# Which units of the first feed-forward network have a slab split for the mixer beside them

## The chip, the cores and the metric

One Trainium2 chip; the program runs on 1 of its cores. The metric is the device time in microseconds (us) of that core, and lower is better. Engines are named as in the profile: PE is TensorE's matrix multiply, PEld its weight load, DVE is VectorE, ACT is ScalarE, POOL is GpSimd, SP is the engine whose queue issues most DMA loads. An engine works through its instructions in the order in which they stand in its program; an instruction that waits holds up those behind it.

## The reference, cut to what matters

One decoder layer on 512 tokens of width 1024, all in float32: a feed-forward half-step (FFN1), a mixer, a second feed-forward half-step (FFN2), a final norm.

```python
x = x + 0.5 * ffn(rmsnorm(x, ffn1_norm), ffn1_w_gate, ffn1_w_up, ffn1_w_down)
x = x + hybrid_mixer(rmsnorm(x, mix_norm), w_in, ..., w_out)
x = x + 0.5 * ffn(rmsnorm(x, ffn2_norm), ffn2_w_gate, ffn2_w_up, ffn2_w_down)
y = rmsnorm(x, final_norm)

def swiglu_ffn(x, w_gate, w_up, w_down):     # w_gate, w_up: 1024x2816, w_down: 2816x1024
    return (silu(x @ w_gate) * (x @ w_up)) @ w_down
```

The mixer multiplies by `w_in` (1024x2048) and `w_out` (1024x1024); what lies between the two does not matter here.

## The kernel before

**Split operands.** Every operand of a product is kept as a rounded part `hi` and a rest `lo`, and every product is three matmuls: hi by hi, hi by lo, lo by hi. A weight slab (128x1024) is loaded as `raw` by SP (L177), cast to `hi` by ACT (L203 or L238), and `lo = raw - hi` is made by DVE (L212). Four `raw` and five `hl` buffers turn over.

**The two feed-forward networks.** The 2816 hidden features are 22 tiles of 128, in groups of 8, 8 and 6 (L21). For each tile j the gate and the up product are made together from seven block products (`seven_units`, L452), each a unit of 12 matmuls that are 256 columns wide; the first tiles are made plainly. The two weight slabs of a pair (gate, up) also give two tiles `tt` of differences (DVE, L226 to L230), so a pair needs four `hl` tiles. The first unit of a pair leaves its product in a PSUM bank; ACT copies it out (L473) and only then the third unit may add to that bank. After each of the first two groups come its down products (`down_a_units`, L538): 8 units, 4 for each half of the output, 24 matmuls of 512 columns each. The last group's down products are `down_b_units` (L564) in FFN1.

**Splits for the mixer.** The mixer's 24 weight slabs (16 of `w_in`, 8 of `w_out`) are split during FFN1, while its own weights stream in, and written to DRAM as hi and lo, from where the mixer loads them later. This is the generator `split_ahead` (L284), which is advanced one step at a time. Step 0 loads slab 0; step n casts slab n-1 on ACT (L290), subtracts on DVE (L291), issues two stores from POOL (L292, L293) and the load of slab n from SP (L296). Loads and halves take their buffers from a pool of 13 (`ACT_BUFS`) that also holds the activations of the group.

```python
for src in srcs[:1] + srcs:                                   # L286
    if raws:
        hi, lo = slot([P, D], "shi", F32R), slot([P, D], "slo", F32R)
        S.copy(hi, raws[-1])                                  # L290, ACT
        V.tensor_sub(lo, raws[-1], hi.bitcast(F32))           # L291, DVE
        G.dma_start(dst[:, 0, :], hi.bitcast(F32))            # L292, POOL queue
        G.dma_start(dst[:, 1, :], lo.bitcast(F32))            # L293
    if len(raws) < len(srcs):
        raws.append(slot([P, D], "sraw"))
        nc.sync.dma_start(raws[-1], srcs[len(raws) - 1])      # L296, SP queue
    yield 1
```

**What sets the order.** `run` (L240) walks a list of units. After each unit that is marked `aside` it advances the generator by one step, with a priority of -400 (L275 to L279); the tile framework then fixes each engine's order from priorities when the kernel is built. Marked are, from tile j = 2 on: the two plain units of j = 2; the fifth unit of each pair whose j is in `BESIDE` (L29, L961); all 8 units of a group's down products (L558, the last argument of `Unit`); and the first 6 units of `down_b_units`. FFN2 runs through the same functions, but the generator is spent by then. 25 steps and one call that ends it are needed; FFN1 before has 31 marked units, so the last ones do nothing.

Of the kernel before, what the change touches and what calls it, by code (L numbers as in the profile page):

```python
# [25 lines left out]
ACT_BUFS = 13  # L26
AHEAD = (8, 4, 3)
PLAIN = (3, 2)
BESIDE = (5, 9, 11, 13, 15, 18, 20)  # L29
ASIDE = 16  # L30
TAPS = 31
PR_NORM = 800
# [40 lines left out]
def layer_kernel(ctx: ExitStack, tc, x, gains, w_g1, w_u1, w_d1a, w_d1b, w_in,  # L73
# [19 lines left out]
    def bank(name):  # L93
        return pb.tile([P, T], F32, name=nm(name), tag="pb")
# [424 lines left out]
    def mm_tok(ps, ahi, alo, whi, wlo, first, last):  # L519
        PE.matmul(ps, ahi, whi, start=first, stop=False)  # L520
        PE.matmul(ps, ahi, wlo, start=False, stop=False)  # L521
        PE.matmul(ps, alo, whi, start=False, stop=last)  # L522

    def add_res(t, oh, ps, scale):
        sl = xt[t][:, oh * 512:(oh + 1) * 512]
        V.scalar_tensor_tensor(out=sl, in0=ps, scalar=scale, in1=sl,
                               op0=ALU.mult, op1=ALU.add)
        dve(0.66)

    def cols(oh):  # L530
        return slice(oh * 512, (oh + 1) * 512)

    def toks(t):
        return slice(t * P, (t + 1) * P)
# [3 lines left out]
    def down_a_units(wd, acts, n):  # L538
        box = {}

        def unit(oh, kp, s):
            if kp == 0:
                box["ps"] = [bank("pd") for _ in range(4)]
            for j in range(2):
                k = 2 * kp + j
                for t in range(4):
                    mm_tok(box["ps"][t], acts[k][:, 0, toks(t)], acts[k][:, 1, toks(t)],
                           s.hi[:, cols(j)], s.lo[:, cols(j)], k == 0, k == n - 1)

        def fin(oh):  # L550
            for t in range(4):
                add_res(t, oh, box["ps"][t], 0.5)

        out_ = []
        for oh in range(2):
            for kp in range(n // 2):
                s = Slab(wd[oh, kp])
                out_.append(Unit([s], 5.44, lambda oh=oh, kp=kp, s=s: unit(oh, kp, s),  # L558
                                 (lambda oh=oh: fin(oh)) if kp == n // 2 - 1 else None, True))
        return out_  # L560


# [377 lines left out]
    def ffn(a0, wg, wu, wd, q, plain, between=()):  # L940
# [8 lines left out]
        for gi, n in enumerate(GROUPS):  # L949
            for i in range(n):  # L950
                j = next(js)
                if j < 2:
                    continue
                if j < plain:
                    put(ffn_units(acts[gi], i, wg[j], wu[j], [ALL]), 1)
                    continue
                if not ready:
                    us.extend(wait(q["name"]))
                    ready = True
                m = seven_units(acts[gi], i, wg[j], wu[j], q)  # L960
                m[4].aside = j in BESIDE  # L961
                if j == FT - 1:
                    put([m[k] for k in (0, 1, 2, 3, 5, 4, 6)], 1)
                else:
                    put(m[:6], 2)
                    late.append(m[6])
            if gi < 2:
                put(down_a_units(wd[gi], acts[gi], n), 1)
            if gi == 0:
                us.extend(between)  # L970
# [129 lines left out]
```

## Time and profile before

| | us |
|---|---|
| median of 3 runs | 879.99 |
| lowest, highest run | 875.72, 881.25 |
| the profiled execution, its own time | 878.23 |
| its span, first to last instruction | 876.4 |
| PE busy | 845.7 (96%) |
| DVE busy | 637.0 (73%) |
| ACT busy | 425.2 (49%) |
| PE's waits for other engines or DMA, longest | 7.1, 6.4 (two waits), 4.0, 1.9 |

The profile is one execution. Times within it count from the first instruction. An engine's busy time is the union of its instructions; a PE that is busy can still run its matmuls closer together or further apart. FFN1 lies at about 18 to 364 us, the mixer at 364 to 520, FFN2 from 526 to the end. A "boundary" below is the point in FFN1 where the down products of a group end and the pairs of the next begin: the first at 144.22 us, the second at 266.52 us.

### The profile page before, as it was taken

Reading aid. Unit: us, or ns where it says so; the run is one execution under the profiler, and the core shown is the slowest. Engines: PE = TensorE matmul, PEld = TensorE weight load, DVE = VectorE, ACT = ScalarE, POOL = GpSimd, SP = SyncE. Lnnn points to the kernel's source line nnn. Section 1 sums busy time; section 2 is a strip of 40 time slices with the busy share of each in tenths; the row PEclk is TensorE's granted clock in tenths of the full one; section 3 lists DMA queues with packets and bytes.
Section 4 is the critical chain, followed back from the end, with each engine's and each line's share of the span. In section 5 each row is a group of like instructions: output and inputs, shape, how many; then the busy total and the mean of one; then the engine's idle time right before and its main releaser. Section 6 shows DMA issues by size and latency. Waiting matters only on the chain.

```text
span 876.4 us, 13745 instructions
## 1 busy us (share of the span) xinstructions
PE 845.7 (96%) x5568; PEld 768.7 (88%) x5568; DVE 637.0 (73%) x899; ACT 425.2 (49%) x677; POOL 89.7 (10%) x112
## 2 busy tenths in 40 slices
PE   7999999999998999999995999999999999999996
PEld 5999987999887998898783789999889999899985
DVE  5989655998666992659988569797547995558844
ACT  7656533656433661436652535555215654135633
POOL 2000011000111000209830010000000000000001
PEclk9999999999999999999998999999999999999998
DMA  7544689555898467555442021234312335223212
GB/s 273 162 134 170 220 309 334 193 193 170 304 325 306 145 230 275 207 202 191 145 156 84 4 93 49 95 104 134 127 49 96 101 117 164 77 73 97 102 44 96
DMA packets 36721, 139.12 MB, mean 159 GB/s; under 512 B 5041, under 2 KB 5169, under 8 KB 33970
## 3 DMA queue, kind: packets, MB, share of 16 engines
q1 hardware_dynamic: 29170, 112.04, 37.8%
q0 software_dynamic: 6912, 25.17, 7.5%
q10 hardware_dynamic: 576, 1.05, 0.3%
q8 instruction: 43, 0.70, 0.3%
q14 instruction: 20, 0.16, 0.1%
HBM read 110.98 MB, written 27.26 MB: 158 GB/s over the span
## 4 chain that ended last, share of the span: by engine, by line
PE 70%; issue 15%; DVE 5%; DMA 4%; ACT 3%; POOL 2%; SPq 0%; POOLq 0%; ACTq 0%; DVEq 0%
PE px L314 19%; PE pz L314 10%; PE pz L305 7%; PE pw L314 5%; PE pd L521 5%; PE pd L520 5%; PE pd L522 5%; PE pgate L305 3%; PE pup L305 3%; DVE pc L659 2%; DMA sraw<-in_w_out 2%; PE po L520 1%; PE po L521 1%; PE po L522 1%; PE pdl L521 1%
## 5 line engine op out<-in xcount | busy, mean ns | idle before, releaser
L212 DVE TENSOR_TENSOR hl<-raw,hl 128x1024 fp32r<-128x1024 f32 (+1 forms) x132 | 139.7, 1062 | 45.4 <-ACT hl L203 33.3
L314 PE MATMUL px<-sx,hl 128*128 128x256 f32 x936 | 122.7, 281 | 6.4 <-ACT sg L473 6.4
L314 PE MATMUL pz<-sx,hl 128*128 128x256 f32 x936 | 121.6, 280 | 0.0
L314 PEld LDWEIGHTS px<-sx,hl 128*128 128x128 f32 x936 | 115.3, 190 | 6.9 <-ACT sg L473 6.9
L520 PE MATMUL pd<-hl,act 128*128 128x512 f32 x304 | 118.7, 390 | 0.0
L521 PE MATMUL pd<-hl,act 128*128 128x512 f32 x304 | 118.4, 390 | 0.0
L522 PE MATMUL pd<-hl,act 128*128 128x512 f32 x304 | 118.4, 389 | 0.0
L212 DVE TENSOR_TENSOR hl<-tt,hl 128x1024 fp32r<-128x1024 f32 x78 | 94.9, 1217 | 30.3 <-ACT hl L238 30.3
L314 PEld LDWEIGHTS pz<-sx,hl 128*128 128x128 f32 x936 | 114.4, 189 | 0.0
L314 PE MATMUL px<-h_hi,hl 128*128 128x256 f32 x624 | 98.0, 280 | 0.0
L238 ACT CAST hl<-tt 128x1024 fp32r<-128x1024 f32 x78 | 81.8, 1052 | 27.8 <-PE pd L522 18.4
L314 PEld LDWEIGHTS px<-h_hi,hl 128*128 128x128 f32 x624 | 84.3, 189 | 1.2 <-DVE um L492 0.6
L203 ACT CAST hl<-raw 128x1024 fp32r<-128x1024 f32 x54 | 56.1, 1052 | 53.0 <-PE pd L522 42.3
L238 ACT CAST hl<-raw 128x1024 fp32r<-128x1024 f32 x78 | 65.1, 835 | 31.8 <-PE pd L522 26.3
L522 PEld LDWEIGHTS pd<-hl,act 128*128 128x128 f32 x304 | 57.1, 188 | 11.8
L520 PEld LDWEIGHTS pd<-hl,act 128*128 128x128 f32 x304 | 57.1, 188 | 11.5
L521 PEld LDWEIGHTS pd<-hl,act 128*128 128x128 f32 x304 | 57.1, 188 | 11.4
L305 PE MATMUL pz<-h_hi,hl 128*128 128x512 f32 (+1 forms) x320 | 64.9, 352 | 0.0
L305 PEld LDWEIGHTS pz<-h_hi,hl 128*128 128x128 f32 x320 | 51.8, 188 | 9.2 <-issue 1.9
L659 DVE SCALAR_TENSOR_TENSOR pc<-sx,ch,pc 128x512 f32<-128x512 f32 x84 | 56.9, 748 | 0.0
L291 DVE TENSOR_TENSOR slo<-sraw,shi 128x1024 fp32r<-128x1024 f32 x24 | 29.3, 1220 | 33.9 <-ACT shi L290 33.9
L290 ACT CAST shi<-sraw 128x1024 fp32r<-128x1024 f32 x24 | 25.2, 1051 | 52.7 <-DMA sraw<-in_w_in 30.3
(181 smaller groups left out, 1346.5 us busy)
## 6 DMA issues: line engine op xcount, KB each, us to landing
raw<-in_w_g SPq DMA_DIRECT2D x44, 512.0 KB, 3.6
raw<-in_w_u SPq DMA_DIRECT2D x44, 512.0 KB, 3.6
hl<-wsi SPq DMA_DIRECT2D x16, 1024.0 KB, 4.8
sraw<-in_w_in SPq DMA_DIRECT2D x16, 512.0 KB, 6.2
wsi<-shi POOLq DMA_DIRECT2D x16, 512.0 KB, 4.7
wsi<-slo POOLq DMA_DIRECT2D x16, 512.0 KB, 5.1
raw<-in_w_d1a SPq DMA_DIRECT2D x16, 512.0 KB, 4.3
raw<-in_w_d2a SPq DMA_DIRECT2D x16, 512.0 KB, 3.5
```

Of the source, the lines that this page charges most:

```text
L203: S.copy(s.hi, s.raw)
L212: V.tensor_sub(s.lo, s.raw, s.hi.bitcast(F32))
L238: S.copy(s.hi, s.raw)
L290: S.copy(hi, raws[-1])
L291: V.tensor_sub(lo, raws[-1], hi.bitcast(F32))
L305: PE.matmul(ps, w[:, k, :], h[:, k, t0:t0 + n], start=(i == 0 and k == 0), stop=(i == 2 and k == KT - 1))
L314: PE.matmul(ps[:, 0:HT], w[:, k * P:(k + 1) * P], h[:, k, :], start=(first and i == 0 and k == 0), stop=(i == 2 and k == 3), skip_group_ch ...
L520: PE.matmul(ps, ahi, whi, start=first, stop=False)
L521: PE.matmul(ps, ahi, wlo, start=False, stop=False)
L522: PE.matmul(ps, alo, whi, start=False, stop=last)
L659: V.scalar_tensor_tensor(out=o if j == TAPS - 2 else to, in0=src, scalar=par(c, P_DW + j), in1=to, op0=ALU.mult, op1=ALU.add)
```

## The change

The marks move; nothing is computed otherwise. `BESIDE` has two more entries, 4 and 6, so those two pairs of the first group get a step. The last two units of the second half of a group's down products lose theirs: the last argument of `Unit` is now true for the whole first half, and for the first two units of the second.

```diff
-BESIDE = (5, 9, 11, 13, 15, 18, 20)
+BESIDE = (4, 5, 6, 9, 11, 13, 15, 18, 20)
@@ down_a_units
                 out_.append(Unit([s], 5.44, lambda oh=oh, kp=kp, s=s: unit(oh, kp, s),
-                                 (lambda oh=oh: fin(oh)) if kp == n // 2 - 1 else None, True))
+                                 (lambda oh=oh: fin(oh)) if kp == n // 2 - 1 else None,
+                                 oh == 0 or kp < n // 2 - 2))
```

## Rows read from the trace of the kernel before

**Rows 1.** PE waits, 100 to 340 us (us in total, times, longest us)
```profile
PE px L314 <- ACT sg L473: 6.4, 2, 4.3
```

**Rows 2.** PE timeline, first boundary (start us, us, instructions, [idle before <-releaser])
```profile
145.63 1.58 PE L314 MATMUL pz<-sx,hl 128*128 128x256 f32 x12
...
149.33 1.65 PE L314 MATMUL px<-sx,hl 128*128 128x256 f32 x12 [2.12 <-ACT sg L473]
...
150.82 0.62 PE L314 MATMUL pw<-h_hi,hl 128*128 128x256 f32 x4
```

**Rows 3.** ACT timeline at the first boundary
```profile
140.87 1.05 ACT L290 CAST shi<-sraw 128x1024 fp32r<-128x1024 f32 x1 [1.80 <-DMA sraw<-in_w_in]
...
147.02 1.04 ACT L290 CAST shi<-sraw 128x1024 fp32r<-128x1024 f32 x1 [4.15 <-DMA sraw<-in_w_in]
...
148.92 0.36 ACT L473 COPY sg<-px 128x256 f32<-128x256 f32 x1
```

**Rows 4.** SP queue timeline, loads issued ahead of the first boundary
```profile
140.88 1.11 SPq L296 DMA_DIRECT2D sraw<-in_w_in  x2
```

**Rows 5.** PE timeline at the second boundary
```profile
267.94 1.58 PE L314 MATMUL pz<-sx,hl 128*128 128x256 f32 x12
...
273.83 2.64 PE L314 MATMUL px<-sx,hl 128*128 128x256 f32 x12 [4.32 <-ACT sg L473]
...
278.30 1.52 PE L314 MATMUL pz<-sx,hl 128*128 128x256 f32 x12
```

**Rows 6.** ACT timeline at the second boundary
```profile
260.80 1.06 ACT L290 CAST shi<-sraw 128x1024 fp32r<-128x1024 f32 x1 [0.72 <-DMA sraw<-in_w_out]
...
272.46 1.04 ACT L290 CAST shi<-sraw 128x1024 fp32r<-128x1024 f32 x1 [1.80 <-DMA sraw<-in_w_out]
```

**Rows 7.** windows: us, busy us per engine (x instructions), PEclk, DMA share, GB/s
```profile
144.22:221.53 77.31, 75.19 (x661) 74.98 (x660) 70.03 (x103) 48.68 (x83) 4.25 (x8) 1.00 0.60 208
...
654.47:732.20 77.73, 77.73 (x661) 77.73 (x660) 64.06 (x94) 45.72 (x78) 0.00 (x0) 1.00 0.32 102
...
266.52:330.70 64.18, 59.86 (x507) 59.29 (x506) 54.88 (x78) 37.71 (x62) 4.56 (x10) 0.97 0.63 225
...
777.19:837.05 59.86, 59.86 (x508) 59.66 (x506) 48.03 (x70) 34.34 (x58) 0.00 (x0) 1.00 0.31 106
...
274.00:277.60 3.60, 3.60 (x19) 3.60 (x20) 2.84 (x3) 1.14 (x3) 0.80 (x2) 0.53 0.84 332
```

**Rows 8.** windows of 10 us, one after a short wait, one without
```profile
30.00:40.00 10.00, 10.00 (x91) 10.00 (x90) 9.57 (x14) 7.54 (x12) 0.00 (x0) 1.00 0.21 79
...
60.00:70.00 10.00, 10.00 (x87) 10.00 (x86) 8.57 (x14) 6.99 (x12) 0.00 (x0) 1.00 0.33 105
```

**Rows 9.** PE timeline of a short wait in the first units
```profile
29.28 0.73 PE L305 MATMUL pgate<-h_hi,hl 128*128 128x256 f32 x4 [0.24 <-ACT h_hi L353]
```

**Rows 10.** instructions and DMA of the tile sraw, all 24 splits
```profile
L291 DVE TENSOR_TENSOR slo<-sraw,shi x24: 1209/1220/1226, 46.6 to 320.8; 128x1024 fp32r<-128x1024 f32 x24
...
DMA to landing us min/median/max: 4.2/6.2/10.0
```

**Rows 11.** DVE timeline, the pairs j=5 and j=6 of the first group
```profile
74.41 0.69 DVE L498 TENSOR_TENSOR sg<-sg,um 128x512 f32<-128x512 f32 x1 [0.73 <-ACT sg L497]
...
84.50 0.68 DVE L498 TENSOR_TENSOR sg<-sg,um 128x512 f32<-128x512 f32 x1
...
87.32 1.21 DVE L212 TENSOR_TENSOR hl<-tt,hl 128x1024 fp32r<-128x1024 f32 x1
```

**Rows 12.** chain that ended last, PE pieces of the same stretch
```profile
90.92 1.41 PE pz L314 x12
```

**Rows 13.** SP queue timeline, the same stretch
```profile
79.98 0.74 SPq L296 DMA_DIRECT2D sraw<-in_w_in  x1
...
86.50 15.22 SPq L177 DMA_DIRECT2D raw<-in_w_d1a  x6
```

**Rows 14.** windows, last down products of the first FFN
```profile
340.00:350.00 10.00, 10.00 (x46) 8.27 (x45) 0.00 (x0) 0.00 (x0) 0.00 (x0) 1.00 0.57 209
```
## The prediction

> **What bounds the kernel now.** The time table comes first: PE is busy for 96% of the span, so only two things can pay, a wait of PE or the pace of its matmuls. The list of PE's waits is next. In the stretch that the change touches it has one entry: a product into `px` waits twice for ACT's copy L473, 6.4 us together, 4.3 the longest [rows 1]. The PE timeline places the two, one at each boundary. At the first, PE has run the first two units of pair j = 8 and the third stands for 2.12 us until 149.33 [rows 2]; at the second it stands 4.32 us until 273.83 [rows 5].
>
> The ACT timeline says why. The copy at 148.92 stood behind a split's cast at 147.02, which had itself idled 4.15 us for the landing of `sraw` [rows 3]. That load had been issued from SP at 140.88 or just after [rows 4]: some 6 us to land, the median of all 24 being 6.2 and the longest 10.0 [rows 10]. At the second boundary the same holds, with the cast at 272.46 [rows 6]. These casts belong to the last split beside a group's down products. The splits cannot keep up there: each needs the one before to free its buffers, then a load. At the first boundary the split before it is cast at 140.87 [rows 3]; at the second, the last one that the change keeps beside the down products is cast at 260.80 [rows 6], 7 us before PE starts the second unit.
>
> The windows give the second thing to see, which the list of waits cannot show. The stretch from the first boundary to the group's down products is 55 units of 12 matmuls. It takes 77.31 us with the wait in it. The same 55 units in FFN2, where no wait occurs, take 77.73 us [rows 7]. So PE ran faster after its wait: by the first timeline, 52 units from 150.82 [rows 2] to 221.53 [rows 7] are 70.71 us, 1.360 each or 113 ns a matmul, against 77.73 / 55 = 1.413 or 118 ns. The granted clock is 1.00 in both windows, so this is not the clock. Nor is it the place: the first group of FFN1, without a wait, shows 87 matmuls per 10 us, and the stretch from 30 us, right after a wait of only 0.24 us [rows 9], shows 91 [rows 8]. The pace is set when PE enters a stretch of 256-column matmuls: coming without a pause from 512-column ones it is the slow pace, restarted after it had run dry it is the fast one, and it keeps it until the next 512-column unit.
>
> **The change part by part.** Count the steps. Marked units before: 2 + 7 + 16 + 6 = 31; after: 2 + 9 + 12 + 6 = 29, still over the 26 calls that are needed, so all 24 slabs are still split. In the first group steps 2 to 4 go beside j = 4, 5, 6, and steps 5 to 10 beside the first six down units; step 11 is beside j = 9 as before. In the second group the down units have steps 15 to 20, j = 18 and 20 have 21 and 22, and steps 23 and 24 (the last two slabs of `w_out`) move into the first two units of `down_b_units`, where step 25 ended the generator before or nothing was left. Nothing is added or taken away: 24 casts, 24 subtractions of 1.22 us [rows 10], 48 stores and 24 loads.
>
> *Taken away at the first boundary.* From the start of unit 2 at 145.63 to the start of unit 4 at 150.82 are 5.19 us for two units that cost 2.83 without a wait: 2.36 us go. *And its price:* the 52 units behind it go back to the slow pace, 52 x (1.413 - 1.360) = 2.78 us. Sum: 0.42 us slower, which is also 77.73 - 77.31.
>
> *Taken away at the second boundary.* From 267.94 to 278.30 are 10.36 us for three units that cost 4.24 without a wait: 6.12 us go. It is more than the 4.32 us of the wait because the granted clock fell after it: 0.53 over the 3.6 us from 274 [rows 7], nearly all of it at the 1.2 GHz level, after PE had stood since about 269.5. The price, for the units behind it, is taken from FFN2's equal stretch: 64.18 against 59.86 us [rows 7], so 4.32 us go in all, 6.12 less 1.80 for the pace.
>
> Sum: 4.32 - 0.42 = 3.90 us.
>
> The pace is where a rule differs. The Trainium skill, TensorE: Matmul & The Clock Gate, section Back-to-back issue gap, gives a single gap for a width and a clock, N / 2.4 + 2.5 ns, 109 ns for 256 columns, whatever ran before. By that rule both pauses would go at no price and the sum would be 8.48 us; the two windows of FFN1 and FFN2, 113 against 118 ns at a granted clock of 1.00, disagree, and I take the rows.
>
> *Added in the first group* (j = 4 and 6, with j = 5 three pairs running): one cast and one subtraction each. In a pair without a split DVE idles 0.73 us ahead of L498; in the pair of j = 5, with one, it idles nothing there [rows 11]. So three splits in a row can make DVE late by a few tenths each. What hides it is the lead with which operands are ready: the `lo` of the `tt` tile that starts at 87.32 and takes 1.21 us [rows 11] is used by the unit at 90.92 [rows 12], 2.4 us later. I cost it at nothing; if the lead were gone it would be at most 2 x 1.22 = 2.44 us, less what a restart at the fast pace returns. Their loads join SP's queue between the raw loads of the pairs; there are fewer activations in the pool of 13 at that time than beside the down products.
>
> *Added in `down_b_units`*: two steps. From 340 to 350 us DVE and ACT are wholly idle and the DMA engines busy for 0.57 [rows 14]; that hides two casts, two subtractions and 3 MB of DMA. Nothing, and if it slipped behind that gap, one cast and one subtraction before the mixer's norm, about 2.3 us.
>
> *What moves on the queues:* two loads (SP) and four stores (POOL) of each of the two groups leave the end of the down products. The load of the next pair's slabs behind them can only come sooner.
>
> The sum is made against the profiled execution: 878.23 - 3.90 = **874.3 us**. The median of the runs shown is 1.76 us above that execution, and the three runs spread over 5.5 us, so I do not shift it.
>
> **The rivals.**
>
> *The pauses go, and the fast pace stays or comes back.* Either the pace has another cause than the restart, or a short wait is left at a boundary: 0.24 us was enough for it once [rows 9], and the splits kept are close to the boundary. With no wait and the fast pace: 2.36 + 6.12 = 8.48 us, 869.8 us. With 0.5 us left at each: 7.5 us, 870.7 us. Against it stands FFN2: two boundaries, no wait at either, slow pace at both. If only the second keeps one, of 1 us: group two saves 6.1 - 1.0 = 5.1, the first loses 0.4, 873.5 us, no different from the forecast. The rule of the Trainium skill quoted above (same page and section) would lead to the 869.8; the rows so far do not bear it out.
>
> *Only the second boundary keeps its wait.* Its splits would have to run two units behind. The row at 260.80 speaks against it. 878.23 + 0.42 = 878.7 us. The change doing nothing at all, because the scheduler places the splits late whichever unit they hang on (their priority is -400), would give 878.2.
>
> *Slower: the split beside j = 6 becomes the new wait.* A step now follows the one before by one pair, 9.9 us, and its load must land in that time. Before, the load of that place was issued at 79.98, with six `raw` loads behind it that took SP's queue from 86.50 to 101.7 [rows 13]. The fifth unit of j = 6 starts three units before the one at 90.92 [rows 12], at about 86.7, and the cast goes with it. Issued at 79.98 the load lands at 86.2 by the median, 90.0 at the longest, and the copy L473 is due two units after 90.92, at 93.7, so nothing happens. It decides against the change if the load falls behind the first two of those six, that is after about 90: landing at 96, copy at about 99, PE stands 5 us and loses some clock too, about 6.1 us as at the second boundary. 878.23 - 3.90 + 6.1 = 880.4 us.
>
> **How the numbers follow.** The forecast 0.55, range of its own 873 to 877 (the offset to the median and 1 us either way for the DMA). Pace kept or a short wait left, 870 to 871: 0.18. A boundary kept or nothing changed, 878 to 879: 0.14. A new wait in the first group, 880 to 882: 0.08. More than one place lost, beyond 882: 0.05. The range 869.7 to 879.0 holds the first three less a part of their scatter, about 0.8. One per cent is about what a measurement of this kernel can tell from no change: faster by over 1% means under 871.2 us, which is the second case, 0.18; slower by over 1% is over 888.8 us, 0.05; within 1% the rest, 0.77.
>
> **What would show it.** Right: no wait of PE for L473 between 100 and 340 us; granted clock 1.00 at the second boundary; the stretches from the boundaries 77.7 and about 59.9 us long, with 87 matmuls per 10 us. Wrong: 91 per 10 us after a boundary without a wait (the pace has another cause); a cast L290 followed by a late L473 near 93 us, or anywhere in j = 4 to 7; ACT waiting for `sraw` before the norm at about 350 us; a wait left at a boundary.

## The result, and the profile after

The changed kernel takes 873.91 us, the median of nine runs (869.83 to 875.16); the kernel before, run beside it, takes 879.99 us (nine runs, 875.72 to 884.28). The ratio is 0.9929, with an interval of 0.9902 to 0.9956: 0.7% faster, within 1%. Two more series of the same changed kernel gave 0.9915 and 0.9940 (below). The profiled execution took 874.41 us against 878.23, so 3.82 us went, 3.90 were forecast. The medians lie further apart, 6.1 us, and the sum does not contain that.

The page's busy line, the kernel after:

```profile
PE 849.3 (97%) x5568; PEld 772.7 (89%) x5568; DVE 638.0 (73%) x899; ACT 425.6 (49%) x677; POOL 89.6 (10%) x112
```

PE is busy for 3.6 us longer than before in a span that is 4.0 us shorter: the same matmuls, fewer pauses, each a little further from the next.

The list of PE's waits for other engines, over the whole span (us in total, times, longest):

```profile
PE pm L640 <- DVE cv L664: 7.0, 1, 7.0
PE g L893 <- DMA grow<-in_gains: 4.1, 1, 4.1
PE ptr L348 <- DVE xn L334: 1.5, 1, 1.5
```

The entry of [rows 1] is gone; what is left stood in the list before too. Between 40 and 340 us there is no entry at all.

The PE timeline at the first and at the second boundary (start, us, instructions):

```profile
145.61 1.58 PE L314 MATMUL pz<-sx,hl 128*128 128x256 f32 x12
147.02 1.58 PE L314 MATMUL px<-sx,hl 128*128 128x256 f32 x12
148.44 0.64 PE L314 MATMUL pw<-h_hi,hl 128*128 128x256 f32 x4
...
268.33 1.58 PE L314 MATMUL pz<-sx,hl 128*128 128x256 f32 x12
269.74 1.58 PE L314 MATMUL px<-sx,hl 128*128 128x256 f32 x12
```

and the ACT timeline around both (in brackets the idle time before, and its releaser):

```profile
137.43 1.05 ACT L290 CAST shi<-sraw 128x1024 fp32r<-128x1024 f32 x1 [7.12 <-DMA sraw<-in_w_in]
...
145.81 0.37 ACT L473 COPY sg<-px 128x256 f32<-128x256 f32 x1 [0.32 <-PE px L314]
...
262.00 1.06 ACT L290 CAST shi<-sraw 128x1024 fp32r<-128x1024 f32 x1 [0.33 <-DMA sraw<-in_w_out]
...
268.53 0.37 ACT L473 COPY sg<-px 128x256 f32<-128x256 f32 x1 [0.32 <-PE px L314]
```

The third unit follows the second at 147.02, after 1.41 us, where in [rows 2] it stood until 149.33; at the second boundary it follows at 269.74, where in [rows 5] it stood until 273.83. The copy L473 now waits for PE alone. The last split's cast is 8.4 us ahead of the copy at the first boundary and 6.5 us at the second, where it had been 1.9 us ahead at the first [rows 3] and 1.0 us at the second, there with nothing between the two.

The windows that answer to [rows 7] and [rows 8] (us, busy us of PE, PEld, DVE, ACT, POOL with instructions, granted clock, DMA share, GB/s):

```profile
144.20:221.93 77.73, 77.73 (x662) 77.73 (x660) 67.06 (x97) 48.27 (x82) 3.19 (x6) 1.00 0.48 165
266.92:326.78 59.86, 59.86 (x508) 59.66 (x506) 51.40 (x74) 36.05 (x60) 2.44 (x6) 1.00 0.59 203
280.00:290.00 10.00, 10.00 (x87) 10.00 (x86) 8.88 (x13) 5.87 (x11) 0.00 (x0) 1.00 0.35 107
274.00:277.60 3.60, 3.60 (x33) 3.60 (x32) 3.60 (x7) 1.74 (x3) 0.00 (x0) 1.00 0.46 151
340.00:350.00 10.00, 10.00 (x46) 8.29 (x45) 4.08 (x6) 2.71 (x4) 1.85 (x4) 1.00 0.79 326
```

Both stretches are now, to a hundredth, as long as their twins in FFN2 of the kernel before [rows 7], 77.73 and 59.86 us; the stretch that ran at a granted clock of 0.53 has 1.00; and the pace behind the boundary is 87 matmuls in 10 us. The last row is the place where two splits more now run: DVE and ACT, idle there before [rows 14], do 4.08 and 2.71 us of work, and PE is busy throughout.

### The profile page after: what moved, and what is told of

Read it like the earlier page. It is cut to its first block, busy times and chain, and to the rows that moved or that the text cites. A ratio compares the mean times of both kernels' runs of the same rounds, so it can differ in the third digit from the quotient of the medians.

```text
span 872.4 us, 13745 instructions
## 1 busy us (share of the span) xinstructions
PE 849.3 (97%) x5568; PEld 772.7 (89%) x5568; DVE 638.0 (73%) x899; ACT 425.6 (49%) x677; POOL 89.6 (10%) x112
## 4 chain that ended last, share of the span: by engine, by line
PE 91%; DVE 4%; ACT 3%; DMA 1%; issue 1%; POOL 0%; SPq 0%; POOLq 0%; ACTq 0%; DVEq 0%
PE px L314 25%; PE pz L314 13%; PE pd L521 8%; PE pd L520 8%; PE pd L522 8%; PE pz L305 7%; PE pw L314 6%; PE pgate L305 3%; PE pup L305 3%; DVE pc L660 2%; PE po L520 1%; PE po L522 1%; PE po L521 1%; PE pdl L520 1%; PE pdl L521 1%; PE pdl L522 1%
## 5 line engine op out<-in xcount | busy, mean ns | idle before, releaser
L291 DVE TENSOR_TENSOR slo<-sraw,shi 128x1024 fp32r<-128x1024 f32 x24 | 29.3, 1222 | 29.6 <-ACT shi L290 29.5
L498 DVE TENSOR_TENSOR sg<-sg,um 128x512 f32<-128x512 f32 x39 | 27.0, 691 | 32.5 <-ACT sg L497 32.5
```

Of the source, the lines that this page charges most:

```text
L498: V.tensor_mul(s, s, box["m"])
```

## The experiments

Two things were in doubt. First, which part of the change brings the gain. Second, the rule of the prediction that a PE which has run dry comes back at the fast pace (1.360 us a unit, 113 ns a matmul) and a PE that comes without a pause runs at the slow one (1.413 us, 118 ns). The rival is that the pace has another cause, and the wait only went with it by chance.

**The same kernel again, twice.** No edit; the longer series of the changed kernel that the others are compared with.

> The changed kernel once more, to have a second profile of it. If the pace of the gate/up pairs is set by how PE enters them, both stretches behind the boundaries are again 77.7 and 59.9 us with no wait in them, and the span is 872.4 us within 1 us. Its nine runs lay in two clusters, 870 and 874 us: if a profile of the lower cluster comes, one of the stretches of 256-column matmuls must be seen to run at 113 instead of 118 ns, or another wait must be shorter by about 4 us.

> The changed kernel, beside the next two for a comparison on one chip: 874 us or 870 us a run, by whether the 635 matmuls of FFN2's first group, which PE enters after a wait of 1.8 us, draw the slow pace or the fast one (2.9 us).

Measured: 874.12 us, ratio 0.9915 (0.9884 to 0.9947), and 873.43 us, ratio 0.9940 (0.9916 to 0.9964). In both profiles every group runs at the slow pace and no wait of PE stands at a boundary. A pause-free boundary gave the slow pace in each of three profiles; for the boundaries that half of the rule stands. The other half does not: FFN2 begins behind a wait of 1.5 us for its norm (`ptr` in the list of waits above), and its first group is slow in all three.

**One boundary at a time.** `e_only1` is the changed kernel with the second group's last two marks put back, `e_only2` the kernel before with only that group's last two marks taken away.

```diff
-                                 oh == 0 or kp < n // 2 - 2))
+                                 oh == 0 or kp < n // 2 - 2 or not drop))
-                put(down_a_units(wd[gi], acts[gi], n), 1)
+                put(down_a_units(wd[gi], acts[gi], n, gi == 0), 1)   # e_only1; gi == 1 in e_only2
```

> The changed kernel with the marks of the second group's last two down units put back: only the first boundary is relieved. The list of waits of PE between 100 and 340 us has one entry, at the second boundary, of 4 us or so; the stretch behind the first boundary is 77.7 us. Against the kernel before: 2.4 us less wait, less what the fast pace had returned there (2.8 us if drawn every time, half of it if drawn every other time): between +0.4 and -1 us, 879 to 880.

> The kernel before with the marks of the second group's last two down units taken away alone: only the second boundary is relieved, the first group has its old places. One wait of some 2 us is left, at the first boundary; the stretch behind the second is 59.9 us. Against the kernel before: 6.1 us less wait and clock, less 1.9 us of pace if it had been drawn every time: -4.3 to -5.2 us, 875 us. If instead both boundaries are worth about the same, -3 us each for this one and the last.

Measured: the first boundary alone 876.72 us, ratio 0.9991 (0.9969 to 1.0012); the second alone 871.06 us, ratio 0.9921 (0.9890 to 0.9952). The windows of the two stretches, `e_only1`:

```profile
143.54:221.27 77.73, 77.73 (x661) 77.73 (x660) 67.38 (x98) 48.28 (x82) 3.20 (x6) 1.00 0.49 167
266.26:331.44 65.18, 61.61 (x508) 61.21 (x506) 54.54 (x77) 37.83 (x62) 4.57 (x10) 0.97 0.61 220
```

a window further behind the wait, of `e_only1` and then of the kernel before:

```profile
281.00:291.00 10.00, 10.00 (x87) 10.00 (x87) 8.46 (x12) 5.76 (x10) 0.00 (x0) 1.00 0.24 84
...
280.00:290.00 10.00, 10.00 (x91) 10.00 (x90) 8.35 (x14) 6.60 (x12) 0.00 (x0) 1.00 0.25 80
```

and the two stretches of `e_only2`:

```profile
144.27:221.39 77.12, 75.20 (x662) 74.99 (x660) 69.95 (x103) 48.73 (x83) 4.26 (x8) 1.00 0.60 206
266.37:326.20 59.83, 59.83 (x507) 59.63 (x506) 50.28 (x72) 36.06 (x60) 2.45 (x6) 1.00 0.57 193
```

The gain sits at the second boundary, as the sum had it (-4.32 against +0.42), but the sizes differ: the medians are 0.5 and 6.2 us under the kernel before (877.26), and the second is outside its expectation of 4.3 to 5.2. Two marks taken away in the second group alone, without the two new pairs, are worth as much as the whole change. In `e_only2` the first stretch with its wait of 1.9 us is even 0.6 us shorter than the clean 77.73. But `e_only1` has something the rule does not allow. Its second boundary keeps a wait of 3.6 us with the clock drop behind it, and yet the 61.61 us of busy time are not those of the fast pace: 10 us from 281 hold 87 matmuls, where the kernel before has 91 after its wait at the same place. Running dry did not bring the fast pace here.

**The two new pairs alone.** The kernel before with 4 and 6 added to `BESIDE`; the marks at the end of the down products stay.

> The kernel before with j = 4 and 6 marked as well and all down units still marked: the other half of the change alone. All 24 splits are then done before the last pairs, and the splits beside the last down units stay. If what lies beside the last two down units is the cause, both waits of PE for L473 are still there, 6 to 7 us together, and the time is that of the kernel before within 1 us. If more splits ahead of the first down products were what helped, the first boundary would be free.

Measured: 878.19 us, ratio 1.0021 (0.9989 to 1.0053). Both waits are still there, 6.0 us together. Windows of the two stretches and of 10 us behind each restart:

```profile
142.37:224.34 81.97, 79.54 (x662) 79.33 (x660) 70.69 (x102) 49.02 (x83) 4.28 (x8) 0.98 0.55 192
269.33:333.64 64.31, 60.75 (x507) 60.18 (x506) 53.48 (x76) 36.11 (x60) 2.44 (x6) 0.95 0.49 175
...
151.67:161.67 10.00, 10.00 (x87) 10.00 (x86) 8.60 (x14) 4.99 (x11) 0.00 (x0) 1.00 0.32 107
281.35:291.35 10.00, 10.00 (x91) 10.00 (x90) 8.01 (x14) 5.84 (x11) 0.00 (x0) 1.00 0.20 73
```

In one execution the restart gave the slow pace at the first boundary (87) and the fast one at the second (91). Where it is slow the wait is paid in full: 81.97 against 77.73, 4.24 us for a wait of 2.43 us and a drop of the clock.

**The marks alone.** The changed kernel with `BESIDE` as it was before: the splits that the down units no longer hold have no new place in the first group, and all shift towards the end.

```diff
-BESIDE = (4, 5, 6, 9, 11, 13, 15, 18, 20)
+BESIDE = (5, 9, 11, 13, 15, 18, 20)
```

> Only the second half of the change: no split beside the last two down units of a group, but no more pairs with one (j = 4 and 6 have none). The splits move to the next marked units, four of them into the last down products. If what counts is what lies beside the last two down units, both boundaries are free of waits, and the time is that of the changed kernel within 1 us; the two extra pairs are then only a place for the splits. If the last four splits come too late there, PE or ACT waits before the mixer's norm, some 1 to 3 us more.

Measured: 881.01 us, ratio 1.0003 (0.9982 to 1.0024), and 6.9 us above the changed kernel in the same series (874.12). Both boundaries are free (the stretches are 77.74 and 59.83 us), so the gain was lost elsewhere. It went ahead of the mixer's norm. The timelines of ACT, DVE and PE there, `e_unmark`:

```profile
350.04 1.05 ACT L290 CAST shi<-sraw 128x1024 fp32r<-128x1024 f32 x1 [6.61 <-DMA sraw<-in_w_out]
...
351.12 1.23 DVE L291 TENSOR_TENSOR slo<-sraw,shi 128x1024 fp32r<-128x1024 f32 x1 [6.43 <-ACT shi L290]
352.26 2.48 DVE L526 SCALAR_TENSOR_TENSOR xt<-pd,xt 128x512 f32<-128x512 f32 x4
...
357.13 1.97 PE L348 MATMUL ptr<-ident,xn 128*128 128x128 f32 x8 [4.21 <-DVE xn L334]
```

and the windows of `e_unmark`, while the load is under way and behind PE's wait:

```profile
340.00:350.00 10.00, 10.00 (x45) 8.28 (x45) 1.42 (x2) 1.05 (x1) 1.59 (x3) 1.00 1.03 423
...
357.00:362.00 5.00, 4.87 (x16) 4.25 (x17) 2.65 (x4) 1.17 (x2) 0.72 (x2) 0.53 0.78 324
```

The last split's load is issued by SP at 337.72 and cast only at 350.04, 12.3 us later, while the DMA engines move 423 GB/s. DVE stands at L291 behind that cast, and the residual sums L526, which the mixer's norm needs, stand behind DVE. PE waits 4.21 us and then runs at a granted clock of 0.53. In the changed kernel the last cast is over before all that begins; its ACT timeline:

```profile
339.67 1.05 ACT L290 CAST shi<-sraw 128x1024 fp32r<-128x1024 f32 x1 [6.63 <-DMA sraw<-in_w_out]
347.72 1.06 ACT L324 ACTIVATE xn<-xt 128x1024 f32<-128x1024 f32 x1 [7.00 <-DVE xt L526]
```

So neither half is worth much alone: the new pairs gain nothing, and the marks, taken away in both groups, give back what they gain. With the new pairs the splits are done early enough. With only the second group's marks away (`e_only2`) the new pairs are not needed.

**A pause put in on purpose.** If running dry gives the fast pace, a short deliberate pause should too. The second and third unit of a pair change places: the third unit adds to the bank that the first left, so it must wait for ACT's copy, and with no unit between them PE stands about 0.5 us. The order of the pair's units is pinned; nothing is left out.

```diff
+        if pause:
+            units[1], units[2] = units[2], units[1]
...
+                start = j == first_seven[gi] and (q["name"], gi) in PAUSE
+                m = seven_units(acts[gi], i, wg[j], wu[j], q, start, start)
```

`e_pause2` does this in the first pair of FFN1's second and third group, `e_pause6` in the first pair of all six groups, `e_pauseall` in all 39 pairs.

> The changed kernel, but in the first pair of FFN1's second and third group the third unit (which has to wait for ACT's copy of the first) is put ahead of the second, so that PE runs dry for about 0.6 us at each boundary. Pace set by a restart: the 54 and 36 units behind go from 1.413 to 1.360 us, -2.9 and -1.9 us, less about 0.7 us for each pause: the stretches 75.6 and 58.7 us, the time 3.4 us under that of the changed kernel. Pace of another origin (the length of the old waits, the clock drop after the second, the traffic of the splits): no unit gets faster, the two pauses cost 1.3 us.

> The same at the start of all six groups, three in each feed-forward network. Pace set by a restart: saves 1.0, 2.2 and 1.2 us in FFN1 and 1.4, 2.2 and 1.2 us in FFN2 (33, 54, 36, 40, 54, 36 units at 0.053 us, less 0.7 us each), together 9.2 us under the changed kernel, about 865 us. Otherwise 4 us more than the changed kernel, and no faster pace in FFN2, where no splits run.

> The third unit ahead of the second in all 39 pairs of both networks, so that PE runs dry for about 0.5 us once in each pair: 39 draws of the pace in one profile. If a restart always gave the fast pace, as the prediction had it, all pairs run at 113 ns a matmul: 39 x (0.7 - 7 x 0.053) = +13 us against the changed kernel. If a restart only draws one of the two paces anew (3 of 6 groups were fast in the run with six pauses, 1 of 2 in that with two), some 15 to 25 of the 39 are fast and it is about +20 us. If the pace belongs to the place, the pairs of one group all show the same pace and those of FFN2's second and third group are slow.

Measured: `e_pause2` 872.84 us, ratio 0.9909 (0.9873 to 0.9945); `e_pause6` 874.03 us, 0.9916 (0.9882 to 0.9949), where 865 was expected; `e_pauseall` 890.55 us (two runs), 1.0156 (1.0098 to 1.0214). Against the changed kernel (874.12) `e_pause2` gained 1.3 us where 3.4 were expected. The pauses came as built, 0.46 us each at the boundaries; the pace did not. The stretch behind the first boundary, `e_pause2`:

```profile
143.53:219.14 75.61, 75.15 (x662) 74.94 (x660) 66.47 (x97) 47.74 (x82) 3.19 (x6) 1.00 0.49 168
```

and `e_pause6`, the same place with the same pause:

```profile
143.49:221.96 78.47, 78.01 (x661) 77.80 (x660) 66.95 (x97) 48.25 (x82) 3.19 (x6) 1.00 0.47 162
...
304.00:314.00 10.00, 10.00 (x91) 10.00 (x90) 9.59 (x16) 6.55 (x12) 0.00 (x0) 1.00 0.44 141
314.00:324.00 10.00, 10.00 (x87) 10.00 (x86) 8.30 (x11) 5.80 (x11) 1.38 (x4) 1.00 0.92 317
```

One restart was followed by the fast pace (75.15 us busy), the other by the slow one (78.01). Of eight such pauses in the two kernels four gave the fast pace. The last two rows show a third thing that the rule denies: a fast stream fell back to the slow pace at about 315 us, in 256-column matmuls and with no wait. In `e_pauseall` the list of waits has 37 pauses (in the last pair of each network another unit falls between the two). FFN1's first group became fast behind its first pause, FFN2's was fast before it, and the four later groups became fast behind their second: 33 pauses of 37 were followed by the fast pace. Each pause cost more than the pace gave back: 0.5 us of standing alone, against 7 x 0.053 = 0.37.

**Pauses in other pairs.** From that pattern, `e_mixa` pauses in the first pair of the first groups and in the first two pairs of the second groups; `e_mixb` in the first pair of the first groups, and only in the second pair of the second and third groups.

```diff
-                start = j == first_seven[gi] and (q["name"], gi) in PAUSE
+                start = (j - first_seven[gi], gi) in ((0, 0), (0, 1), (1, 1))   # e_mixa
+                start = (j - first_seven[gi], gi) in ((0, 0), (1, 1), (1, 2))   # e_mixb
```

> The changed kernel with the swapped order (a pause of PE of about 0.5 us, 0.73 us in all) in the first pair of the first groups and in the first two pairs of the second groups of both networks. In the run with pauses in all pairs the pace was fast behind the first pause of both first groups and behind the second of both second groups, and stayed fast. If that repeats: FFN1 first group -1.0 us, each second group 47 units x 0.053 - 2 x 0.73 = -1.0 us, FFN2's first group -1.4 us or, where its draw was fast anyway, +0.7: 2 to 4 us under the changed kernel. If the draw is free each time, no better than it.

> As the last, but the second and third groups have one pause alone, in their second pair. If a pause in the second pair gives the fast pace whatever came before: 47 and 29 units x 0.053 - 0.73 us, -1.8 and -0.8 us in each network, together with the first groups 5 to 8 us under the changed kernel. If it was the two pauses in a row that gave it, these groups stay slow and cost 0.7 us each, 3 us in all, and the time is that of the changed kernel or 1 us more.

Measured: `e_mixa` 874.06 us, ratio 0.9947 (0.9925 to 0.9969): both first groups fast, both second groups slow after either pause. `e_mixb` 864.22 us (863.10 to 865.39), ratio 0.9837 (0.9812 to 0.9862). The changed kernel itself stood at 873.43 in the same series (`after_third`), so this is 9.2 us below it (5 to 8 were expected), and faster than both kernels of this study. Windows of the two stretches of FFN1 and the two of FFN2, `e_mixb`:

```profile
142.02:217.49 75.47, 75.47 (x662) 75.27 (x660) 67.23 (x98) 47.74 (x82) 3.19 (x6) 1.00 0.52 173
262.47:321.10 58.63, 58.63 (x508) 58.23 (x506) 50.04 (x73) 35.93 (x60) 2.44 (x6) 1.00 0.57 195
642.83:718.30 75.47, 75.47 (x662) 75.27 (x660) 63.88 (x94) 45.70 (x78) 0.00 (x0) 1.00 0.32 104
763.28:821.76 58.48, 58.48 (x508) 57.92 (x506) 48.14 (x70) 34.32 (x58) 0.00 (x0) 1.00 0.34 109
...
301.00:311.00 10.00, 10.00 (x91) 10.00 (x90) 9.60 (x15) 6.53 (x12) 0.53 (x1) 1.00 0.48 127
311.00:321.00 10.00, 10.00 (x86) 9.80 (x85) 7.29 (x11) 6.32 (x10) 0.84 (x3) 1.00 0.98 346
```

All six groups reach the fast pace; FFN2's first had it before its pause, and FFN1's third lost it at 311 us (last two rows). Against 77.73 and 59.86 the four stretches save 2.26, 1.23, 2.26 and 1.38 us. The PE and the ACT timeline at the pause of the second group, `e_mixb`:

```profile
151.44 1.10 PE L315 MATMUL px<-h_hi,hl 128*128 128x256 f32 x8
152.54 1.65 PE L315 MATMUL px<-sx,hl 128*128 128x256 f32 x12
...
152.11 0.37 ACT L476 COPY sg<-px 128x256 f32<-128x256 f32 x1 [1.41 <-PE px L315]
```

In this pair four matmuls of another unit fall between the first and the third. The first row is eight matmuls, and the third unit starts 1.10 us after them, where eight at the slow pace take 0.94: PE loses 0.16 us, too little to be in the list of waits. So `e_mixb` differs from `e_mixa` in two things, the place of the pauses and the length of the later ones, and the runs do not part the two.

## Why the prediction was right, and where it was not

*What bounds the kernel.* Right. The two waits for L473 were late splits, and they went with the marks: the casts L290 lie 8.4 and 6.5 us before the copies, no wait is left, and the second boundary has its granted clock back.

*The two prices.* The first boundary was to lose 0.42 us and the second to gain 4.32. The stretches went from 77.31 to 77.73 and from 64.18 to 59.86 [rows 7], exactly that. The runs with one boundary each, 0.9991 and 0.9921, put the gain where the sum put it. Pricing a wait by an equal stretch without one, rather than by the wait's own length, is what kept the forecast from 869.8 us, the time by which both waits would have gone free of charge.

*The first group.* Right at nothing. The casts of the new pairs have no wait before them and the product behind DVE's L498 keeps its lead; the kernel with the two pairs alone is at 1.0021. The rival of a new wait beside j = 6 did not occur: its load landed at 85.2 us, and the cast ran at 87.46, 3.5 us ahead of the next copy.

*The down products of FFN1.* Right at nothing, but the price named for the case that the cover is gone was too small. Cast and subtraction were put at about 2.3 us. `e_unmark` has the case: from the end of the last pairs to the mixer's first pair it takes 6.6 us more than the changed kernel (325.98 to 366.62 us against 326.78 to 360.78), 5.8 us of span (878.2 against 872.4), because what slips is a load under full DMA traffic, 12.3 us from issue to cast, with DVE standing behind it, and PE restarting at a lower clock. The cover needed there is time for the DMA, not idle time of DVE and ACT.

*The pace.* This is the step that failed, though the sum does not show it. "Restarted after it had run dry it is the fast one, and it keeps it until the next 512-column unit" is false in both parts. The trace of the kernel before already held a case against the first part. PE restarts there at 533.67 us after the 1.5 us wait of FFN2's norm, and the 256-column matmuls behind it are slow (an entry of its list of waits, and a window):

```profile
PE ptr L348 <- DVE xn L334: 1.5, 1, 1.5
...
540.00:550.00 10.00, 10.00 (x87) 10.00 (x86) 9.57 (x13) 5.66 (x9) 0.00 (x0) 1.00 0.08 25
```

In the thirteen profiles this restart was followed by the fast pace five times. The waits that came by themselves at the boundaries of the kernel before, `e_only1`, `e_only2` and `e_beside` were followed by it four times of six. Pauses in the first pair of a second or third group gave it twice in twelve (`e_pause2`, `e_pause6`, `e_mixa`, `e_pauseall`), and pauses in the first pair of a first group that was slow six times of six. In the second pair of a later group they gave it four times of four in `e_mixb` and in `e_pauseall`, but not once of two in `e_mixa`. Twice a fast stream fell back without a wait, at about 315 us in `e_pause6` and 311 us in `e_mixb`, with a DMA share of 0.92 and 0.98 in the 10 us that follow; in the kernel before, 0.88 at the same place left it fast. Both fell behind the same matmul of the program, the 421st of the group, 0.45 us after the same load (`tt<-wso`) was issued from SP. Behind that matmul the next came 128 ns later in both. In the kernel before and in `e_beside` it came 131 and 125 ns later at the same count, and there the pace was back at 113 ns some eight matmuls on. What holds, at the boundaries, is the other half: the three profiles of the changed kernel, which never ran dry at a boundary, show the slow pace at every one. The Trainium skill, *TensorE: Matmul & The Clock Gate*, section *Back-to-back issue gap*, gives 109 ns at 256 columns as the isolated gap of a matmul, and says that in a stream of weight loads and matmuls the spacing is set by both. The runs show two spacings that each last for hundreds of matmuls at a granted clock of 1.00, 113 and 118 ns. Taken as the pace of a stream, as the prediction took it, the one gap would have led to the rival of 869.8.

*What that does to the number.* The forecast of the time does not hang on the pace behind the two waits, because each stretch was put at the length of its twin without a wait; the difference to the kernel before does. The profile of the kernel before happened to have the fast pace behind both waits, which was luck. At a boundary where the restart comes out slow, the wait costs all of its 2.36 or 6.12 us, as the first stretch of `e_beside` shows (4.24 us, none of it given back). With both fast the change is worth 3.9 us, with both slow 2.36 + 6.12 = 8.5. With the four in six counted above it is (2.36 - 0.67 x 2.78) + (6.12 - 0.67 x 1.80) = 5.4 us, and the medians differ by 6.1 us. That the runs without a profile have such a mixture, and that it makes the kernel before scatter over 8.6 us, fits but is argued: only profiled executions show a pace. The profile of before is one draw, and the sum made against it was right for that draw. The time itself had luck too: FFN2's first group was slow in the profiles of both kernels. From its restart to the end of its pairs the fast pace takes 72.9 us (`e_only1`, 534.40 to 607.28), the slow one 75.7 us (changed kernel, 529.74 to 605.43); that would fit the runs of the changed kernel near 870 us, but no profile of such a run was taken. What decides which pace a restart brings stays open: the pauses of `e_pause2` and `e_pause6` at 145.5 us are alike to a hundredth (0.46 us each) and came out differently.

## What to carry to other kernels

Price a wait by an equal stretch that has none, clock and pace included, since against this profile a wait of 2.1 us was worth -0.4 and one of 4.3 us +4.3; and treat a single profile as one draw where the pace behind a wait can come out in two ways. When background work is moved later, look for time in which its loads can land, not for idle engines alone. Where a long stream of equal matmuls runs at the slower of two paces, pauses of 0.2 to 0.5 us can be worth nine in all (864.2 against 873.4 us). Which places work was found by trial: other places gave nothing (`e_mixa`, 874.1 us), a pause in every pair cost more than it gave (`e_pauseall`, 13 us above the kernel before), and no run shows why.

## What the runs showed of the hardware that was not expected

A stream of 256-column matmuls has two steady gaps, 113 and 118 ns, at a granted clock of 1.00. Between gate and up pairs it was seen to change to the shorter gap only where PE had paused, by as little as 0.16 us (`e_mixb`), and among the plain units also behind a wait of 0.24 us [rows 9]. In the first units of a network it changed without a wait too, across eight 128-column transposes (118 to 113 ns at 24.6 us in `e_unmark`). It was seen to change to the longer gap without any wait inside the pairs twice, at the same matmul of the program and each time across one spacing of 128 ns; whether the DMA traffic there (a share of 0.92 and 0.98 in the 10 us that follow) is the cause was not tried. A 0.5 MB load took 12.3 us from issue to the use of its data while the core moved 423 GB/s, against a longest of 10.0 us in [rows 10].
